# Eight weight buffers, each 32 bytes longer, in a one-core mLSTM and sparse-attention block

## The chip, the core and the metric

The kernel runs on one core of a Trainium2 chip. The metric is the device time of one execution in microseconds. Beside it stands one profiled execution of the same program, from which all durations are taken.

## What is computed

One decoder layer on 512 tokens of width 1024, all in float32. The part of the reference that fills most of the time is matrix products:

```python
hN = _rmsnorm(x, norm_g[l])
p = _split_in(hN @ w_in[l])                 # 1024 x 8992, eighteen column groups
...
mh = _mlstm(mq, mk, mv, i, f)               # 4 heads x 256, chunkwise
yn = _nsa(q_raw, q_rope, kc, vc, ks, vs, kw, vw, gates)   # 8 heads x 64
...
merged = (jax.nn.sigmoid(p["g_a"]) * (ya @ w_branch_a[l])
          + jax.nn.sigmoid(p["g_b"]) * (yb @ w_branch_b[l]))
x = x + merged @ w_out[l]
return _rmsnorm(x, final_norm_g)
```

## The kernel before

Each float32 operand of a large product is held as two tiles of type fp32r: a high part and a low part (the operand minus its high part). A product is the sum of three matmuls: high by high, high by low, low by high. ScalarE makes the high part, VectorE the low part; the helper `split` issues both. The normed input, turned, is `hTh` and `hTl` (8 slices of 128 by 512).

**The eight buffers.** The high parts of weights go to the tag `wh`, the low parts to the tag `wl`, four buffers each, in the pool `wp`, which also holds the raw weights (`wr`, three buffers). Each buffer is 1024 float32 per partition, 4096 bytes. `weights` loads raw weights by a DMA on SP's queue and splits them; `hilo` splits quarters of a matrix that are already in SBUF (tiles `R`, and their sums `T`); close to the end a pair of pairs (`w3`) is allocated by hand. A high part and its low part are allocated together, so that they take buffers of the same number.

**Two kinds of large product.** They differ in which operand stands and which moves.

- In `passes`, used by `cols` (columns of `w_in`) and `branch` (the two branch projections), the weights are the stationary operand (128 columns) and the activations move (512 columns): `hTh`, `hTl`, `hTh` for a column job; `yah`, `yal`, `yah` for branch A; `ybh`, `ybl`, `ybh` for branch B. In the profile these are the groups `pp<-hTh,wh` and the like: moving operand first, stationary second.
- In `product`, used by `winograd` (three times: the values, the output gate and the z path) and at the end for `w_out`, the weights move and the activations or their sums stand (`ps<-wh,hTh` and so on). One product has 2 token blocks x 4 slices x 3 matmuls, 24 in all; slices 0 and 1 come from the first pair of weight buffers, slices 2 and 3 from the second. One `winograd` has seven products.

**Order.** `Stream` keeps a queue of `passes` jobs whose matmuls are stepped in between the work of the attention and of the mLSTM heads, so that TensorE always has something to do. The order in time is: norm and small projections (matmuls of 288 columns, moving operands `shi` and `slo`), three Winograd passes with column jobs in between, compression and attention, the mLSTM heads with branch B, branch A, the output product, and the last norm.

**Where the buffers lie.** The compiled program carries each buffer's address within a partition. Here they are for the operands of large products, with the remainder by 256.

| buffers | address | remainder by 256 |
|---|---|---|
| `hTh`, `hTl` | 10176, 26560 | 192 |
| `wh`, four | 61376, 65472, 69568, 73664 | 192 each |
| `wl`, four | 77760, 81856, 85952, 90048 | 192 each |
| `wr`, three | 94144, 98240, 102336 | 192 each |
| `yah`, `yal` | 106432, 122816 | 192 |
| `ybl`, `ybh` | 211904, 221152 | 192, 224 |
| `shi`, `slo` | 183392, 192608 (slices of 1152 bytes) | 96, 224, 96, ... by slice |

Slices of `hTh` and the like are 2048 bytes apart and the stationary slices of weights 512 or 1024 bytes, so a slice keeps its buffer's remainder.

Of the kernel before, what the change touches and what calls it, by code (L numbers as in the profile page):

```python
# [11 lines left out]
F32 = mybir.dt.float32  # L12
F32R = mybir.dt.float32r
# [50 lines left out]
def build(  # L64
# [28 lines left out]
    wp = ctx.enter_context(tc.tile_pool(name="wp", bufs=2))  # L93
# [11 lines left out]
    def f(ap):  # L105
        return ap.bitcast(F32)
# [15 lines left out]
    def split(src, hi, lo, eng="a"):  # L122
        if eng == "a":
            A(hi, src, AF.Copy)
        elif eng == "p":
            pool.tensor_scalar(hi, src, 1.0, 1.0, OP.mult, OP.mult)
        else:
            dve.tensor_copy(hi, src)
        dve.tensor_tensor(lo, src, f(hi), OP.subtract)
# [3 lines left out]
    pending = deque()  # L133
    lazy = []

    def weights(src, eng="a"):
        nk, n = src.shape[1], src.shape[2]
        raw = wp.tile([128, nk, n], F32, name="wr", tag="wr", bufs=3)
        nc.sync.dma_start(raw, src)
        hi = wp.tile([128, nk, n], F32R, name="wh", tag="wh", bufs=4)  # L140
        lo = wp.tile([128, nk, n], F32R, name="wl", tag="wl", bufs=4)
        if lazy:
            pending.append(lambda: split(raw, hi, lo, eng))
        else:
            split(raw, hi, lo, eng)
        return hi, lo

    def wcols(c0):
        return weights(wv[:, :, c0 : c0 + 128])

    def wwide(view, c0):
        ws = [weights(view[:, k : k + 4, c0 : c0 + 256]) for k in (0, 4)]
        return (lambda k: ws[k // 4][0][:, k % 4, :]), (lambda k: ws[k // 4][1][:, k % 4, :])
# [125 lines left out]
    def hilo(qs):  # L279
        out = []  # L280
        for q in qs:
            hi = wp.tile([128, 2, 512], F32R, name="wh", tag="wh", bufs=4)
            lo = wp.tile([128, 2, 512], F32R, name="wl", tag="wl", bufs=4)
            split(q, hi, lo)
            out.append((hi, lo))
        return out

    with tc.tile_pool(name="ph0", bufs=2, side="right") as p0, tc.tile_pool(
        name="small", bufs=1, side="right"
# [77 lines left out]
        def evacuate(tb, ps):  # L367
            pv = ps[:, 0:256].rearrange("p (b g d) -> p b g d", b=2, g=2)
            split(pv, vsw[:, tb, :, :, 0, :], vsw[:, tb, :, :, 1, :])
            dve.tensor_tensor(gp[:, tb], ps[:, 256:288], bias, OP.add)  # L370
# [24 lines left out]
        def low(tb, hf):  # L395
            ks = slice(hf * 4, hf * 4 + 4)
            dve.tensor_tensor(
                hTl[:, ks, blk[tb]], banks[tb, hf], f(hTh[:, ks, blk[tb]]), OP.subtract
            )
# [98 lines left out]
        for hf in range(2):  # L498
            high(3, hf)
            low(3, hf)  # L500
        w1 = hilo(vq[0, 0])
        evacuate(1, sums[1])
        for tb in (3, 2):
            for hf in (1, 0):
# [33 lines left out]
    for i, k in enumerate(("A11", "A12", "A21", "A22")):  # L538
        r, c = slice(i // 2 * 256, i // 2 * 256 + 256), slice(i % 2 * 4, i % 2 * 4 + 4)
# [38 lines left out]
    def winograd(qs, target, sink, between=(), w1=None):  # L578
# [21 lines left out]
        b11, b21, b12, b22 = qs[0, 0], qs[1, 0], qs[0, 1], qs[1, 1]  # L600
        X = [PS() for _ in range(2)]
        product(X, "A11", w1 or hilo(b11))
        do("P1")
        a = keep(X, "ka")
        Z = [PP() for _ in range(2)]
        w2 = hilo(b21)
        t3 = plus(WS(), b12, b22)
        do("t3")
# [620 lines left out]
    for n in range(NT, last + NT + BEHIND):  # L1229
        u, m = n // NT, n - NT - BEHIND  # L1230
        if n % NT == 0:
            if u % 4 == 3 and u < 15:
                c = u // 4 + 1
# [78 lines left out]
    def branch(base, j, yh, yl, nk):  # L1312
        def gen(w):
            o = 0 if nk == ND else (j % 2) * 128
            ps = PP()
            yield from passes(
                ps, lambda k: w[0][:, k, o : o + 128], lambda k: w[1][:, k, o : o + 128],
                lambda k: yh[:, k], lambda k: yl[:, k], nk,
            )
            s = halves.pop((base, j))  # L1320
            if base == GB:
                if not merged:
                    merged.append(pers.tile([128, ND, T], F32, name="mB", tag="hTh"))
                dve.scalar_tensor_tensor(merged[0][:, j], s, 1.0, ps, OP.add, OP.mult)
            else:
                keep(dve.scalar_tensor_tensor(s, s, 1.0, ps, OP.add, OP.mult))
                merge(j, s)

        def load():
            halves[base, j] = sgp.tile([128, T], F32, name="s", tag="s")  # L1330
            nc.sync.dma_start(halves[base, j], gD[base, j])
            if nk == ND:
                return weights(wav[:, :, j * 128 : j * 128 + 128])
            if j % 2 == 0:
                halves["w"] = weights(wbv[:, :, j * 128 : j * 128 + 256])
            return halves["w"]

        stream.add(load, gen)
# [32 lines left out]
    for h in range(4):  # L1371
# [5 lines left out]
        for sb in range(NT):  # L1377
            o, n = KOFF[sb], 512 - sb * 128
# [78 lines left out]
    with tc.tile_pool(name="fin", bufs=1, reuse_waits="tile") as fp:  # L1457
# [4 lines left out]
        for i, k in enumerate(("M11", "M12", "M21", "M22")):  # L1462
            r, c = slice(i // 2 * 256, i // 2 * 256 + 256), slice(i % 2 * 4, i % 2 * 4 + 4)
# [40 lines left out]
        def tiles(tag, bufs):  # L1504
            return [fp.tile([128, 2, 512], F32, name=tag, tag=tag, bufs=bufs) for _ in range(2)]

        def load(i, j, ts):
            for n, t in enumerate(ts):
                ks = slice(i * 4 + n * 2, i * 4 + n * 2 + 2)
                nc.sync.dma_start(t, wov[:, ks, j * 512 : j * 512 + 512])  # L1510
            return ts
# [8 lines left out]
        b22 = load(1, 1, tiles("R", 8))  # L1520
# [35 lines left out]
        def join(tb, cs, bank, scale=0.5):  # L1556
            xv = xo[:, tb, cs]
            dve.scalar_tensor_tensor(xv, bank, scale, xv, OP.mult, OP.add)
# [64 lines left out]
        for i in range(2):  # L1623
# [15 lines left out]
        times(2, L)  # L1639
        begin(2)  # L1640
        join(3, L, X[1])
        w3 = [
            tuple(wp.tile([128, 2, 512], F32R, name=t, tag=t, bufs=4) for t in ("wh", "wl"))
            for _ in range(2)
        ]
        for (hi, _), q in zip(w3, b22):
            A(hi, q, AF.Copy)
        square(3, L, 0)
        for (hi, lo), q in zip(w3, b22):
            dve.tensor_tensor(lo, q, f(hi), OP.subtract)  # L1650
            if lo is w3[0][1]:
                join(3, R, X[1], -0.5)
        product(Y[:1], "MS1", w5, tbs=(0,))
        join(2, R, Y[0])
# [67 lines left out]
```

## Time and profile before

| what | value |
|---|---|
| median of the timed runs | 600.15 us (599.79 to 600.52, 2 runs) |
| the profiled execution's own time | 600.57 us |
| its span, first to last instruction | 598.8 us |
| TensorE busy | 590.5 us, 99% of the span |
| VectorE, ScalarE, GpSimd busy | 485.6, 352.4, 79.8 us |
| mean granted TensorE clock | 0.999 |

The span leaves 1.8 us of the execution's time outside. A busy TensorE is not a TensorE at its peak: a matmul's duration in the profile covers its whole passage, and consecutive ones overlap. What a matmul costs in a full stretch is the time from its start to the next one's start, and that is the length of a stretch divided by its count. The chain of work that ended last gives such stretches: each row is a start, a length, and how many instructions it merges. One execution is profiled; its durations are compared with each other, not with a clock outside.

### The profile page before, as it was taken

To read this page: it belongs to the slowest core of one execution; us is meant where nothing else is said; L and a number is where in the kernel's file an instruction comes from. 1 tells how busy PE (TensorE), PEld (TensorE's weight loads), DVE (VectorE), ACT (ScalarE), POOL (GpSimd) and SP (SyncE) were. 2 spreads that over 40 slices of the span, in tenths; PEclk is the share of its full clock that TensorE was granted. 3 is DMA by queue.
4 is the path that set the end of the run, shared out by engine and by line. 5 is a ranking of instruction groups with operands and counts; after the bars stand their busy time and mean duration, and the time that the engine had idled before them with its cause. 6 is when DMAs were issued, how large, how long until landed. Compare 5 with 4: busy or idle time off the path is not lost.

```text
span 598.8 us, 8454 instructions
## 1 busy us (share of the span) xinstructions
PE 590.5 (99%) x2956; PEld 496.1 (83%) x2956; DVE 485.6 (81%) x902; ACT 352.4 (59%) x648; POOL 79.8 (13%) x134
## 2 busy tenths in 40 slices
PE   8999999999999999999999999999999999999995
PEld 7988888888888888888888888888888888888885
DVE  5899689597586889787977776889898978589975
ACT  6854546654457477566666765656566563424564
POOL 3000000000015013223323320001010101010121
PEclk9999999999999999999999999999999999999999
DMA  8945454403046663323133123422232236990633
GB/s 317 338 138 181 153 171 128 153 2 88 15 117 178 154 176 94 89 57 89 41 88 107 36 70 108 140 72 71 70 106 65 63 100 192 325 239 19 210 54 141
DMA packets 83717, 74.17 MB, mean 124 GB/s; under 512 B 3870, under 2 KB 66202, under 8 KB 83675
## 3 DMA queue, kind: packets, MB, share of 16 engines
q1 hardware_dynamic: 82520, 71.14, 39.6%
q0 software_dynamic: 1008, 2.36, 2.1%
q8 instruction: 23, 0.38, 0.3%
q14 instruction: 20, 0.16, 0.1%
q10 hardware_dynamic: 146, 0.14, 0.1%
HBM read 61.36 MB, written 8.45 MB: 117 GB/s over the span
## 4 chain that ended last, share of the span: by engine, by line
PE 83%; DVE 9%; ACT 3%; DMA 2%; issue 1%; POOL 1%; SPq 0%; POOLq 0%; ACTq 0%; DVEq 0%
PE pp L80 50%; PE ps L80 19%; PE pt L80 10%; PE po L80 4%; DVE u L80 4%; DVE wl L80 2%; DMA sraw<-w_small 1%; ACT wh L80 1%; DVE num L80 1%; DMA wr<-w_in 1%; DVE qkl L80 1%; ACT qkh L80 1%; ACT th L80 1%; POOL rho L1404 0%; DVE yal L80 0%
## 5 line engine op out<-in xcount | busy, mean ns | idle before, releaser
L80 PE MATMUL pp<-hTl,wh 128*128 128x512 f32 x352 | 142.2, 404 | 0.0
L80 PE MATMUL pp<-hTh,wh 128*128 128x512 f32 x352 | 139.0, 395 | 0.0
L80 PE MATMUL pp<-hTh,wl 128*128 128x512 f32 x352 | 138.3, 393 | 0.0
L80 DVE TENSOR_TENSOR wl<-wr,wh 128x1024 fp32r<-128x1024 f32 x56 | 69.6, 1246 | 11.1 <-ACT wh L80 11.0
L80 PEld LDWEIGHTS pp<-hTh,wh 128*128 128x128 f32 x352 | 66.2, 188 | 12.8
L80 ACT ACTIVATE wh<-wr 128x1024 fp32r<-128x1024 f32 x56 | 58.3, 1058 | 29.9 <-PE pp L80 17.6
L80 PEld LDWEIGHTS pp<-hTl,wh 128*128 128x128 f32 x352 | 66.3, 188 | 10.6
L80 PEld LDWEIGHTS pp<-hTh,wl 128*128 128x128 f32 x352 | 66.3, 188 | 10.6
L80 ACT ACTIVATE P<-P,st 128x128 f32<-128x128 f32 (+3 forms) x64 | 35.7, 558 | 27.3 <-DVE st L80 27.2
L1148 POOL TENSOR_SCALAR P<-P,st 128x128 f32<-128x128 f32 (+3 forms) x56 | 37.8, 694 | 91.4 <-DVE st L80 59.4
L80 DVE TENSOR_TENSOR wl<-T,wh 128x1024 fp32r<-128x1024 f32 x28 | 34.0, 1222 | 14.0 <-ACT wh L80 13.9
L80 DVE TENSOR_TENSOR wl<-R,wh 128x1024 fp32r<-128x1024 f32 x28 | 33.8, 1220 | 10.6 <-ACT wh L80 10.6
L80 ACT ACTIVATE wh<-T 128x1024 fp32r<-128x1024 f32 x28 | 29.4, 1056 | 18.5 <-PE pp L80 11.2
L80 DVE TENSOR_TENSOR ptl<-pt,pth 128x512 fp32r<-128x512 f32 (+1 forms) x64 | 30.9, 485 | 11.3 <-ACT pth L80 10.5
L80 ACT ACTIVATE pth<-pt 128x512 fp32r<-128x512 f32 (+1 forms) x64 | 27.4, 428 | 20.3 <-PE pt L80 20.0
L80 ACT ACTIVATE wh<-R 128x1024 fp32r<-128x1024 f32 x28 | 29.2, 1056 | 13.9 <-PE pp L80 6.8
L80 DVE SCALAR_TENSOR_TENSOR u<-pp,prm,u 128x511 f32<-128x511 f32 (+2 forms) x48 | 35.5, 742 | 0.7 <-ACT u L80 0.2
L80 DVE CUSTOM_DVE_ANT_0 P<-ps,cst 128x128 f32<-128x128 f32 (+3 forms) x64 | 30.5, 482 | 6.3 <-PE ps L80 6.1
L80 PE MATMUL ps<-k,Th 128*128 128x256 f32 (+2 forms) x112 | 28.4, 336 | 0.0
L80 PE MATMUL pt<-cst,P 128*128 128x128 f32 x160 | 28.1, 272 | 0.0
L80 PEld LDWEIGHTS pt<-cst,P 128*128 128x128 f32 x160 | 20.8, 140 | 7.0 <-DVE ptl L80 0.3
L80 PE MATMUL pp<-yah,wh 128*128 128x512 f32 x64 | 25.0, 390 | 0.0
(354 smaller groups left out, 1362.1 us busy)
## 6 DMA issues: line engine op xcount, KB each, us to landing
wr<-w_in SPq DMA_DIRECT2D x44, 512.0 KB
R<-w_in SPq DMA_DIRECT2D x24, 512.0 KB
gD<-sg SPq DMA_DIRECT2D x16, 256.0 KB
s<-gD SPq DMA_DIRECT2D x16, 256.0 KB
wr<-w_branch_a SPq DMA_DIRECT2D x8, 512.0 KB
R<-w_out SPq DMA_DIRECT2D x8, 512.0 KB
vD<-cq SPq DMA_DIRECT2D x8, 256.0 KB
wr<-vD SPq DMA_DIRECT2D x4, 512.0 KB
```

Of the source, the lines that this page charges most:

```text
L80: ins = fn(*args, **kw)
L1148: pool.tensor_scalar(pj, pj, st[:, 2, j : j + 1], 1.0, OP.mult, OP.mult)
```

## The change

The two tags `wh` and `wl` are allocated 1032 float32 long in place of 1024, and the first 1024 are used, through a helper `high_low`. Each buffer thus takes 4128 bytes, 32 more than before. A tile `gap` of 64 float32 (256 bytes) is allocated once in the same pool behind the first use of the pairs and before the first use of `wr`; nothing reads or writes it. The comparison `lo is w3[0][1]` becomes `q is b22[0]`, which is true at the same place.

```diff
+    def high_low(nk):
+        return [
+            wp.tile([128, 1032], F32R, name=t, tag=t, bufs=4)[:, :1024].rearrange(
+                "p (k c) -> p k c", k=nk
+            )
+            for t in ("wh", "wl")
+        ]
+
     def weights(src, eng="a"):
         nk, n = src.shape[1], src.shape[2]
         raw = wp.tile([128, nk, n], F32, name="wr", tag="wr", bufs=3)
         nc.sync.dma_start(raw, src)
-        hi = wp.tile([128, nk, n], F32R, name="wh", tag="wh", bufs=4)
-        lo = wp.tile([128, nk, n], F32R, name="wl", tag="wl", bufs=4)
+        hi, lo = high_low(nk)
...
         for q in qs:
-            hi = wp.tile([128, 2, 512], F32R, name="wh", tag="wh", bufs=4)
-            lo = wp.tile([128, 2, 512], F32R, name="wl", tag="wl", bufs=4)
+            hi, lo = high_low(2)
             split(q, hi, lo)
...
         w1 = hilo(vq[0, 0])
+        wp.tile([128, 64], F32, name="gap", tag="gap", bufs=1)
         evacuate(1, sums[1])
...
-        w3 = [
-            tuple(wp.tile([128, 2, 512], F32R, name=t, tag=t, bufs=4) for t in ("wh", "wl"))
-            for _ in range(2)
-        ]
+        w3 = [high_low(2) for _ in range(2)]
...
-            if lo is w3[0][1]:
+            if q is b22[0]:
                 join(3, R, X[1], -0.5)
```

If the pool keeps its order (the four `wh`, the four `wl`, the gap, the `wr`), the new addresses follow from the sizes: 61376 + n x 4128 for the `wh`, remainders 192, 224, 0, 32; 77888 + n x 4128 for the `wl`, remainders 64, 96, 128, 160; 94656 for the first `wr`. Everything that lies behind on the same side moves by 8 x 32 + 256 = 512 bytes and keeps its remainder. A high part and its low part then differ by 128 in the remainder, and neighbouring pairs by 32; the first `wh` buffer still has the remainder of the other operands.

## The prediction

> **What bounds the kernel now.** I read the busy table and the 40 slices first, then the chain's shares, then the chain in order of time.
>
> ```profile
> span 598.8 us, 8454 instructions
> PE 590.5 (99%) x2956; PEld 496.1 (83%) x2956; DVE 485.6 (81%) x902; ACT 352.4 (59%) x648; POOL 79.8 (13%) x134
> ...
> PE   8999999999999999999999999999999999999995
> ...
> PEclk9999999999999999999999999999999999999999
> ...
> PE 83%; DVE 9%; ACT 3%; DMA 2%; issue 1%; POOL 1%; SPq 0%; POOLq 0%; ACTq 0%; DVEq 0%
> ```
>
> TensorE is busy in every slice but the first and the last, at full clock, and 83% of the chain is its work. No wait stands out that could be removed. So the time is a number of matmuls times the step from one start to the next, and the change can matter only if it alters that step. The chain's stretches give the step, as length over count:
>
> ```profile
> 12.10 4.26 PE pp L80 x32
> ...
> 31.08 27.20 PE pp L80 x120
> ...
> 96.65 16.32 PE ps L80 x72
> ...
> 364.30 12.10 PE pp L80 x53
> 376.64 10.68 PE pp L80 x47
> ...
> 405.30 12.29 PE pp L80 x54
> ...
> 502.75 6.94 PE pp L80 x30
> ...
> 510.56 43.54 PE pp L80 x192
> ```
>
> The column jobs (120 in 27.20), a Winograd product's stretch (72 in 16.32) and branch A (192 in 43.54) step by 226.7, 226.7 and 226.8 ns. There every operand has remainder 192 by 256, whichever of the two kinds of operand moves. Branch B (30 in 6.94) steps by 231.3 ns; it is the one large product whose operands differ today, `ybh` lying 32 bytes higher than `ybl` and the weights. The first row is the small projections with 288 columns (32 in 4.26): 133.1 ns, with moving slices at 96 and 224 and stationary ones at 192.
>
> To compare 288 columns with 512 I need the step's dependence on columns, from a stretch of 256 columns at equal remainders near the end:
>
> ```profile
> 584.21 0.28 PE L80 MATMUL pp<-wh,mSh 128*128 128x256 f32 x1
> ...
> 586.61 0.28 PE L80 MATMUL pp<-wh,mSl 128*128 128x256 f32 x1
> ...
> 586.73 0.40 PE L80 MATMUL pp<-wh,mSh 128*128 128x512 f32 x1
> ```
>
> From 584.21 to 586.73 there are 21 steps: 2.52 us, 120.0 ns each. So 256 more columns cost 106.7 ns, 0.417 ns a column, and a matmul of 512 columns is 213.4 ns of columns and 13.3 ns that don't depend on them. A straight line puts 288 columns at 133.3 ns; measured are 133.1. The small projections lose nothing by their unequal remainders, and branch B loses 231.3 - 226.8 = 4.5 ns a matmul. These two rows are the only evidence on the change's subject, and they disagree.
>
> **The change part by part.** It adds no instruction, DMA or wait, and moves none: same tags, same number of buffers, same order. It changes addresses: the weight buffers get remainders 192, 224, 0, 32 (high) and 64, 96, 128, 160 (low), all else keeps its own.
>
> *VectorE and ScalarE, which make the parts.* Branch B's split already has an operand that lies 32 off; a head's split has none:
>
> ```profile
> L80 ACT ACTIVATE yb<-oc x4: 625/634/636, 298.6 to 369.0; 128x512 fp32r<-128x512 f32 x4
> L80 DVE TENSOR_TENSOR yb<-oc,yb x4: 673/679/694, 300.2 to 369.7; 128x512 fp32r<-128x512 f32 x4
> ...
> L80 ACT ACTIVATE qkh<-u x16: 613/632/635, 379.4 to 484.7; 128x512 fp32r<-128x512 f32 x16
> L80 DVE TENSOR_TENSOR qkl<-u,qkh x16: 681/691/694, 380.5 to 485.3; 128x512 fp32r<-128x512 f32 x16
> ```
>
> 634 against 632 ns on ScalarE, 679 against 691 on VectorE: zero. If it weren't zero, say 12 ns either way on each of 112 low parts, 1.3 us would spread over an engine that is 81% busy and behind TensorE's cover; should the cover go, 1.3 us is the whole price. The helper views the buffer as slices of a longer row; the values' split writes such a view too (256 used of every 258):
>
> ```profile
> L80 DVE TENSOR_TENSOR vl<-wr,vh x4: 1192/1204/1219, 373.7 to 475.5; 128x1024 fp32r<-128x1024 f32 x4
> ...
> L80 DVE TENSOR_TENSOR wl<-wr,wh x56: 1204/1222/1645, 26.6 to 535.7; 128x1024 fp32r<-128x1024 f32 x56
> ```
>
> 1204 against 1222 ns: zero again. The DMAs of the raw weights land in the same count of bytes at the same remainder, 512 bytes higher: zero. Buffers behind them move by the same 512 bytes; a tile may now overlap another old one by a few hundred bytes more or less, but what lay there was done with long before, so I take zero.
>
> *TensorE's step in `passes`.* There the moving operand stays at 192 and only the stationary one's remainder changes. In the small projections the stationary slice lies 96 and 32 away from the moving one, at no cost. What sets branch B apart from them is the sequence of moving operands: `ybh`, `ybl`, `ybh`, a jump of 32 bytes and back in each three, while successive slices of `shi` lie 128 apart. Two jumps cost 3 x 4.5 = 13.5 ns, 6.8 ns a jump. I take that reading, since it alone fits both rows: a jump of 32 in the moving operand costs, distance to the stationary one doesn't. Then 1344 matmuls of `passes` (three groups of 352, three of 64, 96 of branch B) keep their step.
>
> The Trainium skill, in TensorE: Matmul & The Clock Gate, section "Step-by-step: what each phase is for", goes further: it gives TensorE two independent read ports, so that a load of the next weights takes nothing from the running matmul. By that the change is worth nothing anywhere; branch B's 231.3 ns shows that placement is not quite free.
>
> *TensorE's step in `product`.* Here the weights move: high, low, high of one pair, 128 apart, as the slices of `shi` are; after slice 1 the next pair follows, 32 away, and at the next token block the first one again. That is 4 jumps in each of 28 products (three passes of seven, and seven at the end): 112 x 6.8 ns = 0.8 us. The least is zero; the most, if all 28 x 24 = 672 matmuls run at branch B's 4.5 ns extra, 3.0 us. I take 0.8, because the runs between jumps are six matmuls long and resemble the small projections.
>
> *The sum.* 600.57 us (the profiled execution's own time, 1.8 beyond its span and 0.4 above the median of 600.15) + 0.8 = **601.3 us**, between 600.6 and 603.6 by this reading.
>
> **The rivals.**
>
> *Distance to the stationary operand costs (slower).* In branch B, two of three matmuls have a moving operand 32 from the stationary one: 6.8 ns for each such matmul. After the change 7 of 8 buffers lie off. The quiet matmuls, which step by 226.7 today, are those of these windows and of the three pieces 53, 47 and 54 above:
>
> ```profile
> 30.00:80.00 50.00, 50.00 (x222) 41.31 (x221) 42.21 (x77) 27.59 (x36) 0.00 (x0) 1.00 0.49 149
> 80.00:183.00 103.00, 103.00 (x456) 85.32 (x455) 80.65 (x84) 56.24 (x71) 4.98 (x14) 1.00 0.32 99
> 183.00:360.00 177.00, 177.00 (x964) 149.16 (x963) 142.25 (x369) 116.58 (x281) 48.12 (x68) 1.00 0.37 98
> ...
> 510.00:583.00 73.00, 73.00 (x327) 60.53 (x325) 61.51 (x84) 36.11 (x51) 7.60 (x10) 1.00 0.59 170
> ```
>
> 222 + 456 + 327 + 154 = 1159; times 7/8 times 6.8 ns is 6.9 us: 607.5 us. If the 857 others of the 2016 large matmuls (1344 + 672), those between attention and heads, lose as much, 5.1 us more: 612.6. The small projections speak against it, at 133.1 ns for distances of 32 and 96; branch B for it, though its other explanation is there. It decides from the point where a distance costs anything in `passes`; 2% would need 11.8 ns on each quiet matmul.
>
> *Unequal remainders relieve the interleaved stretches (faster, in part).* In the window from 183 to 360 the large matmuls last longer than the quiet ones, whose median is 389 ns:
>
> ```profile
> L80 PE MATMUL pp<-hTl,wh 128*128 128x512 f32 x352 | 142.2, 404 | 0.0
> L80 PE MATMUL pp<-hTh,wh 128*128 128x512 f32 x352 | 139.0, 395 | 0.0
> L80 PE MATMUL pp<-hTh,wl 128*128 128x512 f32 x352 | 138.3, 393 | 0.0
> ...
> L80 PE MATMUL pp<-yah,wl x64: 389/389/393, 510.9 to 553.7; 128*128 128x512 f32 x64
> ```
>
> 352 x (15 + 6 + 4) ns = 8.8 us would come back: 591.8. Against it: these stretches have the same remainders as the quiet ones, so that the excess goes with the mixing of small matmuls and not with placement.
>
> *The fixed 13.3 ns is a collision of equal remainders (faster, in full).* If moving and stationary reads hold each other up because both start at 192, 7/8 of 2016 matmuls would lose 13.3 ns: 23.5 us, 577.1. Against it stand the two rows with unequal remainders, neither of which steps by less than the line through the equal ones. The Trainium skill, in TensorE: Matmul & The Clock Gate, section "Wait — 56ns, not 53.3ns?", has 215.7 ns between starts at 512 columns; by that figure 11.0 ns a matmul are there to be had, an estimate of 19.4 us or 581.2 in all. The trace has no step so short in any stretch above.
>
> *The change doesn't do what it says.* If the pool rounds 4128 bytes up to a multiple of 256, or places the tags otherwise, remainders stay equal: 600.6, inside the forecast's own range.
>
> **How the numbers follow.** Forecast, no loss in `passes` and little in `product`, with the last rival in it: 0.50, 600.6 to 603.6. Distance costs: 0.27, mostly 605 to 609, with 0.05 beyond 2%. Relief in part: 0.10. Relief in full: 0.07. Left over, mostly a loss at the distances of 64 to 224 that no row shows: 0.06, beyond 2%. A measurement of this kernel tells about 2%, 12 us, from no change, so within 588.1 to 612.2 counts as the same. Faster 0.08 (full relief and a little of the partial one), slower 0.05 + 0.06 = 0.11, same 0.81. The range reaches from the partial relief, 591.8, to 609.5 in the second case; 0.07 lie below and 0.12 above.
>
> **What would show it.** Right: branch A stays at 192 in about 43.5 us, column jobs at 226.7 ns, while stretches of products rise from 226.7 to about 228 (four jumps of 6.8 in 24). The distance rival: branch A's 192 take 44.4 to 44.9 us. Full relief: they take about 41.3. Partial relief: `pp<-hTl,wh` falls from 404 towards 389 ns. VectorE's `wl` rows leaving 1222 ns by more than a few ns would break the zero there. Wrong altogether would be a new wait of TensorE on a buffer, in a stretch that has none today.

## Result and profile after

The changed kernel takes 606.80 us (606.65 to 606.94, 2 runs) against 600.15: a ratio of 1.0111, 95% interval 1.0067 to 1.0154. It is slower by 6.65 us, clear of noise and within 2%. Its profiled execution takes 606.94 us, 6.37 more than that of before. The compiled program has the addresses that follow from the sizes: `wh` at remainders 192, 224, 0, 32, `wl` at 64, 96, 128, 160, all else at its old remainder.

From the page of the changed kernel, span, busy times and the chain's shares:

```profile
span 605.2 us, 8455 instructions
...
PE 597.2 (99%) x2956; PEld 496.3 (82%) x2956; DVE 486.6 (80%) x902; ACT 352.3 (58%) x648; POOL 79.1 (13%) x134
...
PE 96%; ACT 1%; DMA 1%; DVE 1%; issue 1%; POOL 0%; SPq 0%; POOLq 0%; ACTq 0%; DVEq 0%
```

TensorE has 6.7 us more of busy time for the same 2956 matmuls, and every other engine's is the same to about 1 us. No wait has come up: TensorE's share of the chain has risen to 96%. So the step has changed. The chain in order of time (start, length, count):

```profile
25.43 5.55 PE ps L80 x24
30.98 27.88 PE pp L80 x120
...
97.98 16.68 PE ps L80 x72
...
189.71 1.91 PE ps L80 x16
...
367.81 12.37 PE pp L80 x53
...
507.38 6.97 PE pp L80 x30
515.22 44.58 PE pp L80 x192
```

Column jobs step by 27.88 us / 120 = 232.3 ns (226.7 before), the products' stretch by 231.7 (226.7), branch A by 232.2 (226.8). Branch B, slow before, has stayed at 232.3 (231.3). So both kinds of large product have become slow, the one in which the weights stand and the one in which they move.

With two more rows of the chain of the kernel before, both executions can be cut at the same places:

```profile
25.62 5.46 PE ps L80 x24
...
186.41 1.91 PE ps L80 x16
```

| stage, from start to start | before, us | after, us | difference |
|---|---|---|---|
| span's start to the first product | 25.62 | 25.43 | -0.2 |
| Winograd passes and column jobs | 160.79 | 164.28 | +3.5 |
| compression and attention | 177.89 | 178.10 | +0.2 |
| heads and branch B | 146.26 | 147.41 | +1.2 |
| branch A, output product, last norm | 88.24 | 89.98 | +1.7 |

The loss lies where large matmuls follow each other. Where small ones are mixed in, which is most of the attention's stage, there is next to none.

### The profile page after: what moved, and what is told of

The parts are those of the page before. It is cut to its first block, busy times and chain, and to the rows that moved or that the text cites. A ratio compares the mean times of both kernels' runs of the same rounds, so it can differ in the third digit from the quotient of the medians.

```text
span 605.2 us, 8455 instructions
## 1 busy us (share of the span) xinstructions
PE 597.2 (99%) x2956; PEld 496.3 (82%) x2956; DVE 486.6 (80%) x902; ACT 352.3 (58%) x648; POOL 79.1 (13%) x134
## 4 chain that ended last, share of the span: by engine, by line
PE 96%; ACT 1%; DMA 1%; DVE 1%; issue 1%; POOL 0%; SPq 0%; POOLq 0%; ACTq 0%; DVEq 0%
PE pp L80 59%; PE ps L80 21%; PE pt L80 12%; PE po L80 5%; DMA xt<-x 1%; DVE xo L80 0%; ACT junk L80 0%; POOL fr L1583 0%; DVE wl L80 0%; ACT xo L80 0%; ACT sq L80 0%; SPq L316 0%; SPq L317 0%; POOLq L1722 0%; ACT shi L80 0%
## 5 line engine op out<-in xcount | busy, mean ns | idle before, releaser
L80 ACT ACTIVATE wh<-T 128x1024 fp32r<-128x1024 f32 x28 | 29.5, 1056 | 19.4 <-PE pp L80 11.6
L80 PE MATMUL pp<-yah,wl 128*128 128x512 f32 x64 | 25.3, 396 | 0.0
```

What stands on the lines that cost most here:

```text
L80: ins = fn(*args, **kw)
```

## Experiments

Two theories of the loss stood first. **D**: a distance, counted by 256 bytes, between the moving operand and the standing one costs, whatever the neighbours do. **S**: what costs is the change of remainder from one matmul to the next, so that a start can't settle; a constant distance is free. D was the first rival. S is my forecast's reading, widened to both operands: in its own form, where only jumps of the moving operand cost, branch A refutes it already, since there the moving operand stays at 192 and the step is 232.2 ns all the same. In all kernels below that move the buffers as a block, the first lines of the diff are a tile ahead of the first use of `wh`, with a second one behind `wl` where the sum has to come to 256 bytes:

```diff
+        wp.tile([128, N], F32, name="lead", tag="lead", bufs=1)
         w1 = hilo(vq[0, 0])
+        wp.tile([128, 64 - N], F32, name="gap", tag="gap", bufs=1)
```

### A constant distance of 32 and of 128

N is 8 (all eight at remainder 224), then 32 (all eight at 64).

> All eight weight buffers keep 4096 bytes and start 32 bytes later, so that every one has remainder 224 and every other large operand 192: a distance of 32 in each matmul, the same from matmul to matmul. Theory D (a distance between the moving and the stationary operand costs, whatever its neighbours do): every large matmul is off, none has remainder 192 on both sides; branch A's 192 steps take 44.4 to 44.9 us, the total is 606 to 609 us. Theory S (what costs is that the remainder changes from one matmul to the next, so that the start can't settle): nothing changes from matmul to matmul, branch A takes 43.5 us, the total is 600 us.

> All eight weight buffers keep 4096 bytes and start 128 bytes later, remainder 64, a constant distance of 128. Theory D: 606 us or more, as with 32, unless the distance counts by 128 only; branch A 44.4 us or more. Theory S: 600 us, branch A 43.5 us.

Measured: 608.62 us, 1.0135 (1.0120 to 1.0150), and 608.50 us, 1.0133 (1.0116 to 1.0150). The chains, all at 224 first, then all at 64:

```profile
30.75 28.00 PE pp L80 x120
...
98.14 16.80 PE ps L80 x72
...
516.37 44.81 PE pp L80 x192
```

```profile
31.15 27.92 PE pp L80 x120
...
98.49 16.80 PE ps L80 x72
...
516.43 44.62 PE pp L80 x192
```

Every stretch shown is slow, at 232.4 to 233.4 ns a matmul, and no remainder in them changes from one matmul to the next. S falls. These constant distances cost 5.6 to 6.6 ns, in the total more than the mixture of the change does.

### Steps of 64 and of 128 bytes

```diff
-            wp.tile([128, 1032], F32R, name=t, tag=t, bufs=4)[:, :1024].rearrange(
+            wp.tile([128, 1040], F32R, name=t, tag=t, bufs=4)[:, :1024].rearrange(
...
-        wp.tile([128, 64], F32, name="gap", tag="gap", bufs=1)
```

This is against the changed kernel; the second has 1056 in place of 1040.

> Buffers 64 bytes longer each, no gap tile: remainders 192, 0, 64, 128 for the high parts and the same for the low parts, so that a pair is equal and pairs differ by multiples of 64. Theory D with a period of 256: 3/4 of the matmuls are off, 605 us, a quarter of branch A's jobs quiet. Theory S with a period of 256: a change only where the pair changes, once in 24 matmuls in passes and four times a product; nearly 600 to 602 us. Either theory with a period of 64 (only the remainder by 64 counts): 600 us, all stretches at 226.7 ns.

> Buffers 128 bytes longer each, no gap tile: remainders 192, 64, 192, 64 for high and low parts alike. Theory D with a period of 256: half of the matmuls are off, 603.5 us, branch A's jobs alternate between quiet and slow. Theory S: 600 to 601 us. Either with a period of 128 or 64: 600 us, all stretches at 226.7 ns.

Measured: 606.65 us, 1.0101 (1.0086 to 1.0116), and 604.95 us, 1.0076 (1.0061 to 1.0091). Branch A with steps of 64, then with steps of 128:

```profile
515.65 44.35 PE pp L80 x192
```

```profile
514.58 44.11 PE pp L80 x192
```

231.0 ns with three buffers of four off, 229.7 with one of two: about 0.65 and 0.45 of the way from 226.8 to 233.4. The loss goes with the share of buffers that are off, and neither 64 nor 128 is a period. The single starts in the trace show it within one execution: with steps of 128, branch A's eight jobs of 24 matmuls each step by about 227 ns or by 232.2 to 232.7, four jobs of each kind.

### Another address at the same remainder

N is 64, with no gap: every weight buffer 256 bytes later.

> All eight weight buffers keep 4096 bytes and start 256 bytes later: another address for every one of them, the same remainder by 256, another one by 512. Theory D with a period of 256 (distance between moving and stationary operand, counted by 256): 600.5 us, branch A 43.5 us. Rivals: a period of 512, or the move itself (what overlaps what, what lies behind): 606 to 609 us, branch A 44.6 to 44.8 us, as with 32 and 128.

Measured: 600.83 us against 600.80, 0.9998 (0.9989 to 1.0007).

```profile
30.84 27.20 PE pp L80 x120
...
96.40 16.32 PE ps L80 x72
...
510.48 43.54 PE pp L80 x192
```

These stretches are those of before to the hundredth. For a shift of 256 bytes, it is the remainder that counts, not the move.

### Everything 32 later

```diff
+    pers.tile([128, 8], F32, name="lead")
     li = pers.tile([128, NT, 4], F32, name="li")
```

The tile is the first on the left side of memory, where the weights and all large activations but branch B's lie.

> Everything on the left side of memory, weights, activations and sums, starts 32 bytes later: remainder 224 throughout; the distances between them stay zero. Only branch B's ybl, at 192, is now off the weights, ybh is not. Theory D: 600.5 us, branch A 43.5 us, branch B's 30 steps near 6.9 us. Rival (the weights' own remainder of 192 is what is good, or 224 is bad): 608 us as in the run with all weights at 224.

Measured: 600.84 us, 1.0000 (0.9991 to 1.0009).

```profile
503.14 6.99 PE pp L80 x30
511.00 43.55 PE pp L80 x192
```

Weights at 224 are as good as at 192 when the activations lie there too. So it is the distance, not the weights' own place. Branch B's stretch, in which `ybl` alone is now off, takes 6.99 us, against 6.94 with `ybh` off: one matmul in three costs here as much as two in three did, so the loss isn't a fixed price for each matmul that is off.

### The low parts alone

A tile of 128 bytes between the first high and the first low part, and one behind:

```diff
             hi = wp.tile([128, 2, 512], F32R, name="wh", tag="wh", bufs=4)
+            if not mid:
+                mid.append(wp.tile([128, 32], F32, name="mid", tag="mid", bufs=1))
             lo = wp.tile([128, 2, 512], F32R, name="wl", tag="wl", bufs=4)
...
         w1 = hilo(vq[0, 0])
+        wp.tile([128, 32], F32, name="gap", tag="gap", bufs=1)
```

> Only the low parts start 128 bytes later, remainder 64; the high parts stay at 192. One large matmul in three is then off: in passes the one in which the low part stands (or is being loaded), in product the one in which it moves. Theory D with a cost for each matmul by itself: a third of the 8 us of the run with all at 64, 603.2 us, branch A 43.9 us. Theory D with a memory (an off matmul also makes the two after it slow): 605 to 608.5 us, branch A 44.3 to 44.6 us, and the two matmuls with equal remainders step by more than 227 ns.

Measured: 605.71 us, 1.0077 (1.0061 to 1.0092).

```profile
98.44 16.64 PE ps L80 x72
...
515.00 44.38 PE pp L80 x192
559.38 5.49 PE ps L80 x24
```

Branch A steps by 231.1 ns, two thirds of the full loss for one matmul in three that is off. The single starts in the trace say which are slow. Here are branch A's mean steps, from the start of the matmul named to the next one's start:

| matmul | its standing weights | weights loaded meanwhile | step |
|---|---|---|---|
| `yah,wh` | equal | equal | 226.8 ns |
| `yal,wh` | equal | off | 232.6 ns |
| `yah,wl` | off | equal | 234.0 ns |

In the trace the load of the next weights starts some 3 ns after the matmul itself and takes 188 ns, so it is the weights of the third column that are loaded while the matmul runs. Weights that are off in either column make it slow. The memory of the expectation, by which an off matmul slows the two after it, is not what happens, though its total and its time for branch A came true: the matmul ahead of the off one is slow, and the one behind it is not.

In `product` the same pattern gives 231.1 ns in the Winograd stretch (72 in 16.64) and 228.8 in the last products (24 in 5.49). In the last products only the matmul with the off moving operand is slow (234.3 ns against 226.7 and 225.7); in the Winograd stretch all three are (229.4 to 232.9 ns). Why the same remainders give two results is not known.

### Branch B's high part at 192

Made from the kernel before:

```diff
-    ybh = yb[:, 4 * T + 264 :].rearrange("p (c t) -> p c t", c=4)
+    ybh = yb[:, 4 * T + 256 : 8 * T + 256].rearrange("p (c t) -> p c t", c=4)
```

> The kernel before with branch B's high part moved by 32 bytes, so that it has remainder 192 like all other operands of the large products. Theory D: branch B's stretch of 30 matmuls falls from 6.94 to 6.80 us, the 96 matmuls of branch B give back up to 0.4 us, the total is 600.1 us, which a measurement can hardly tell from 600.5. Rival (branch B is slow for another reason, its place beside the last head): 6.94 us as before.

Measured: 600.78 us, 0.9997 (0.9988 to 1.0005).

```profile
503.09 6.82 PE pp L80 x30
510.79 43.56 PE pp L80 x192
```

Branch B's stretch falls from 6.94 to 6.82 us, 227.3 ns a matmul: nearly all of its loss in the kernel before came from its 32 bytes. In the total the 0.1 us of this stretch is lost in the spread. No version here beats the kernel before.

### Is the loss the same at every distance?

N is 48 (all at 128), 56 (all at 160) and 16 (all at 0).

> All eight weight buffers at remainder 128, a constant distance of 64 from the other operands: in passes the moving operand lies 64 above the standing one, in product 64 below. In the run with steps of 64 the matmuls that loaded a weight at 128 stepped by 229.5 ns against 233 for those at 0 and 64. Theory D flat (any distance costs the same 6.7 ns): 608 to 609 us, branch A 44.6 to 44.8 us. Theory D graded (the cost depends on the distance and its sign): branch A near 192 x 229.5 ns = 44.1 us, the total between 603 and 606 us.

> All eight at remainder 160: the moving operand 32 above the standing one in passes, 32 below in product, the mirror of the run with all at 224. Flat: 608.5 us, branch A 44.8 us. Graded: in the changed kernel the matmuls at this distance stepped by 230.3 ns in branch A and 228.6 ns in the last products, so branch A near 44.2 us and the total near 604 us.

> All eight at remainder 0: the moving operand 64 below the standing one in passes, 64 above in product, the mirror of the run with all at 128. Flat: 608 to 609 us, branch A 44.6 to 44.8 us. Graded: 233.1 ns in passes as in the run with steps of 64, branch A 44.7 us, but the products, whose distance is then that of passes in the mirror run, below 5.6 us each.

Measured: 605.76 us, 1.0087 (1.0072 to 1.0102); 609.00 us, 1.0141 (1.0126 to 1.0156); 607.13 us, 1.0110 (1.0093 to 1.0126). The products' stretch and branch A with all at 128, at 160 and at 0:

```profile
97.97 16.80 PE ps L80 x72
...
514.45 43.97 PE pp L80 x192
```

```profile
99.01 16.80 PE ps L80 x72
...
517.01 44.80 PE pp L80 x192
```

```profile
97.92 16.48 PE ps L80 x72
...
515.12 44.81 PE pp L80 x192
559.92 5.60 PE ps L80 x24
```

At a constant distance (moving minus standing remainder) the step of a matmul is:

| distance | passes (branch A) | product (stretch of 72) |
|---|---|---|
| 0 | 226.8 ns | 226.7 ns |
| +32 and -32 | 233.3 and 233.4 | 233.3 and 233.3 |
| 128 | 232.4 | 233.3 |
| -64 | 233.4 | 233.3 |
| +64 | 229.0 | 228.9, but 233.3 in the last products |

The cost is nearly flat, with one exception: a moving operand 64 above the standing one costs a third in `passes` (all at 128) and in the Winograd products (all at 0). This is not a rule of the distance alone. In that last run the products near the end, whose standing operands have remainder 192 too, are at the same distance and take the full 5.60 us for 24. What the two stretches differ in is not known. My graded expectation held for all at 128 and failed for all at 160, where the mixed stretches had looked cheaper than the pure ones are.

## Why the prediction was right and wrong

**The outcome.** 606.8 lies in the range of 591.8 to 609.5 and within 2%, as the largest chance had it. The likeliest case, 601.3 us, did not come; the first rival did, at 607.5, with a chance of 0.27. The range was right because it took in that rival: the mechanism behind the forecast itself was wrong.

**What bounds it, and that only the step can change: right.** TensorE's 99%, the missing waits and the unchanged counts held.

**VectorE and ScalarE at zero: right.** From the changed kernel's instructions on `wl`, minimum, median and maximum:

```profile
L80 DVE TENSOR_TENSOR wl<-wr,wh x56: 1205/1222/1757, 26.4 to 541.3; 128x1024 fp32r<-128x1024 f32 x56
```

The median is 1222 ns again. DMAs and buffers behind: zero, as the run with the same remainders 256 bytes later and that with everything 32 later show.

**The step in `passes`: this is the one that failed.** The forecast had 1344 matmuls keep their step, because a jump of the moving operand costs and a distance doesn't. The constant distance of 32 shows the contrary. The premise was that the small projections lose nothing at unequal remainders, since 133.1 ns lies on the straight line through 256 and 512 columns at equal ones. The runs show two faults in it. First, the small projections did lose: in the run with everything on the left 32 later, half of their matmuls have equal remainders and the others lie 128 apart, and the stretch of 32 that took 4.26 us has become shorter:

```profile
12.42 4.18 PE pp L80 x32
```

These are 130.6 ns a matmul; in all other runs the stretch takes 4.25 or 4.26 us. Second, the line's lower end isn't the fast case. At 256 columns a distance costs nothing and some distances save time: here are the first and the last of 24 such matmuls near the end, with all weights at 224 and then with all at 128.

```profile
591.81 0.28 PE L80 MATMUL pp<-wh,mSh 128*128 128x256 f32 x1
...
594.50 0.28 PE L80 MATMUL pp<-wh,mSl 128*128 128x256 f32 x1
```

```profile
589.05 0.28 PE L80 MATMUL pp<-wh,mSh 128*128 128x256 f32 x1
...
591.66 0.28 PE L80 MATMUL pp<-wh,mSl 128*128 128x256 f32 x1
```

These are 23 steps of 117.0 and 113.5 ns, where equal remainders had 120.0. So a line through equal remainders at two widths is no measure of what a distance costs at a third. Between 288 and 512 columns nothing was tried, so how the loss grows with the width stays open.

**The step in `product`: mis-sized.** The term was four jumps of 6.8 ns in each product, 0.03 us. In the changed kernel a product takes 5.55 to 5.56 us against 5.44, four times that: its 24 matmuls step by 231 ns or more on average, so that not only those at a jump are slow.

**The distance rival: right in mechanism and nearly in price.** It had 6.8 ns for each off matmul and 6.9 us in all. Measured are 5.6 to 6.6 ns at most constant distances and 2.2 ns at the cheapest; the change cost 6.65 us. That its price for one matmul came so close is in part luck: it divided branch B's loss by the matmuls that are off, and the low parts alone show two slow matmuls in `passes` for one that is off. Its second end, 5.1 us more in the interleaved stretches, didn't come: with all at 224, the attention's stage runs from 190.54 to 368.99, 178.45 us against 177.89.

```profile
190.54 1.90 PE ps L80 x16
...
368.99 12.42 PE pp L80 x53
```

**Relief in part and in full: neither.** No stretch of 512-column matmuls shown in any of these kernels steps by less than 226.7 ns, and `pp<-hTl,wh` has a mean of 406 ns in the changed kernel against 404.

```profile
L80 PE MATMUL pp<-hTl,wh 128*128 128x512 f32 x352 | 142.9, 406 | 0.0
L80 PE MATMUL pp<-hTh,wh 128*128 128x512 f32 x352 | 140.0, 398 | 0.0
L80 PE MATMUL pp<-hTh,wl 128*128 128x512 f32 x352 | 139.5, 396 | 0.0
```

At 512 columns the fixed 13.3 ns is therefore no collision of equal remainders. At 256 columns a distance of 64 does take 6.5 ns off the step (113.5 against 120.0), so there the rival's idea isn't excluded.

The rule of the Trainium skill that I quoted from TensorE: Matmul & The Clock Gate, section "Step-by-step: what each phase is for", is that loading the next weights takes nothing from the running matmul. It does not hold to the last 3% here: with the low parts alone moved, a matmul steps by 232.6 ns while an off weight is loaded and by 226.8 while an equal one is, and the measurement decides.

**What is not settled.** That the two reads meet somewhere by address is an inference from the distance; no run shows where, or whether, they do. Nor is it shown why a matmul is slow whose standing weights are off but were loaded before it began, as the low parts' 234.0 ns are.

## What to carry to other kernels

When TensorE is full and no wait is left, divide long stretches of the chain by their counts and compare the steps: a few nanoseconds between stretches of equal shape can point to placement, and one padded tile tests it. For fp32r matmuls of 512 columns like these, keep moving and standing operands at the same remainder by 256 bytes, and give padded tiles a multiple of 256; here 32 bytes a buffer cost 1.1%. Don't carry a cost or its absence from one width of matmul to another: at 256 columns equal remainders were not the fastest.

## What the hardware showed unexpectedly

The loss is not one delay that each matmul gets. At equal remainders branch A's starts are regular to a nanosecond: 226, 227, 227 ns and again. With all weights at 64 the remainders are the same for every matmul, and yet the steps run from 228 to 241 ns in a cycle of seven, such as 241, 232, 231, 232, 228, 230, 232. What sets the cycle was not tried.

At 256 columns the order is another: 113.5 ns with all weights at 128, 117.0 with all at 224, and 120.0 both at equal remainders and at a distance of 128.
